# Rows padded to 128 bytes, and weights at a chosen address modulo 128, in a two-layer trunk on one core

## The chip, the core and the metric

The kernel runs on one core of one Trainium2 chip. The metric is the time of one execution on the device in microseconds (us). Three runs of the kernel before are shown; their median is compared.

## What is computed

Two layers of a decoder trunk over 256 positions of width 1024, in float32. Cut to what matters here:

```python
for l in range(2):
    h = rms_norm(x, norm_mix_pre[l])
    q, k, v, lru_x, lru_gate, glu_in, gates = split(h @ w_in[l])   # 1024 -> 11776
    y_a = dilated_attention(q, k, v) @ w_o_attn[l]     # 3 groups x 8 heads x 64
    y_b = rg_lru(lru_x, lru_gate) @ w_o_lru[l]
    y_c = conformer_conv(glu_in) @ w_o_conv[l]         # depthwise, 31 taps
    x = x + rms_norm((g0*y_a + g1*y_b + g2*y_c) @ w_out[l], norm_mix_post[l])
    u = square(relu(rms_norm(x, norm_mlp_pre[l]) @ w_mlp_up[l]))   # 1024 -> 4096
    x = x + rms_norm(u @ w_mlp_down[l], norm_mlp_post[l])
```

## The kernel before

**Products in three passes.** Each operand of a large product is split into a high part, rounded to the type fp32r (a cast on ScalarE, `act` with Copy, L392), and the remainder (a subtraction on VectorE, `tt`, L405). A product is then high x high, high x low and low x high: three matmuls, all issued at L452 in `matmuls`. Each brings its own load of the stationary operand.

**The stream of weights.** All weight matrices lie in memory as 92 chunks of 1 MiB a layer (128 partitions x 2048 float32). `weights` (L483) takes the next: a DMA on SP's queue into `raw` (two buffers), then `split` in two halves into `whi` and `wlo` (a ring of three buffers each, 8192 bytes a partition). One chunk feeds 48 matmuls of 256 columns or 24 of 512.

**Two forms of product.** In the gemm form (`ws_items`, `gemm`) the weights are the stationary operand, 128 x 128, and the activations move, 256 columns: `lx`, `glu`, `lg`, `q`, `k`, `ga`, `gb`, `gc`, `ob`, `oa`, `oc` and `up`. In the `as` form (`as_items`, `as_gemm`, `vproj`) the activations are stationary and the weights move, 512 columns: `v`, `wo`, `ua` and `dn`. For `v1` and `v2` (the dilated groups) the stationary operand takes every second element. The gates of the recurrent branch (`psr`, `psi`) are of the gemm form, but their weights are split into ordinary slots.

**Where tiles lie.** Three pools follow each other in on-chip memory: `cp` (constants and parameters), `wp` (the weight rings), `sp` (all else). A tile is placed when it is first used, at a multiple of 32 bytes. Activations lie in `hh` and `hl` (the normed input, high and low) or in the 24 slots with tag `s2` (2048 bytes each). In the program as built the first tile of `cp` is at 16512, `raw`, `whi` and `wlo` begin at 32 modulo 128, and `hh`, `hl` and all `s2` slots at 96 modulo 128; the rows of `whi`, `wlo`, `hh`, `hl` and `s2` are multiples of 128 bytes, so this holds for each buffer of a ring.

**One held chunk.** At the end of the first layer `dn61` is called with `spread`: its weights go into eight `s2` slots instead of the rings, half of its matmuls run with the first 128 positions and half later with the other 128. These matmuls have both operands in slots.

**The order of the work.** `Sched.run` simulates the engines with costs written by hand (`op(eng, cost, ...)`, costs by element counts), picks by priority, and emits all instructions in one static order per engine. `ORDER`, `CONV_AT` and `WHERE` (L38 to L44) place the chunks, the convolution's taps and the attention scores. Costs depend on a view's number of elements, not on addresses. The main matmuls follow each other in the order of the chunks; score, transpose and attention matmuls are put in between.

Of the kernel before, what the change touches and what calls it, by code (L numbers as in the profile page):

```python
# [8 lines left out]
F32R = mybir.dt.float32r  # L9
# [4 lines left out]
P = 128  # L14
# [5 lines left out]
CHUNK = 2048  # L20
# [26 lines left out]
def chunk_plan():  # L47
    q0, k0, v0, lx0, lg0, gl0, br0 = 0, 1536, 3072, 4608, 5632, 6656, 8704
    plan = []

    def ws(name, mat, c0, c1=None):
        plan.append((name, "ws", mat, (c0, c0 + P if c1 is None else c1)))

    for n in ORDER:
        kind, a = n[:2], n[2:]
        if n[0] == "v":
            for kb in range(2):
                plan.append((f"{n}{kb}", "as", "w_in", (kb, v0 + int(n[1]) * 512)))
        elif n[0] in "qk":
            plan.append((n, "rope", "w_in", (q0 if n[0] == "q" else k0) + int(n[1]) * 512 + int(n[2]) * 256))  # L60
        elif kind == "gl":
            ws(n, "w_in", gl0 + int(n[3]) * P, gl0 + D + int(n[3]) * P)
        elif kind == "oa":
            plan.append((n, "oa", "w_o_attn", int(a) * 512))
        elif kind != "lw":
            mat, c0 = {"lx": ("w_in", lx0), "lg": ("w_in", lg0), "ga": ("w_in", br0), "gb": ("w_in", br0 + D),
                       "gc": ("w_in", br0 + 2 * D), "ob": ("w_o_lru", 0), "oc": ("w_o_conv", 0)}[kind]
            ws(n, mat, c0 + int(a) * 256)
    for c in range(2):
        for kb in range(2):  # L70
            plan.append((f"wo{c}{kb}", "as", "w_out", (kb, c * 512)))
    for kb in range(9):
        if kb == 0:
            plan += [(f"ua{k}", "as", "w_mlp_up", (k, 0)) for k in range(2)]
        elif kb < 8:
            ws(f"up{2 * kb}", "w_mlp_up", (2 * kb) * 256)
            ws(f"up{2 * kb + 1}", "w_mlp_up", (2 * kb + 1) * 256)
        if kb > 0:
            for c in range(2):
                plan.append((f"dn{kb - 1}{c}", "as", "w_mlp_down", (kb - 1, c * 512)))  # L80
    return plan
# [11 lines left out]
NHI = 3  # L93
# [7 lines left out]
DMA_RATE = 0.36  # L101
MARGIN = 15000
DMA_ISSUE, DMA_START, DMA_DONE = {"SP": 600, "POOL": 1040, "ACT": 600}, 500, 900
RINGS = ("mm", "tp", "sc", "raw", "whi", "wlo", "upad", "xp", "sm", "pT")


class Buf:
    def __init__(self, sch, pool, shape, dt, tag, name):
        self.sch, self.pool, self.shape, self.dt, self.tag, self.name = sch, pool, shape, dt, tag, name
        self.t = None  # L110
        self.log = []
        self.left = 0
        self.held = False
        self.uses = []

    def __getitem__(self, idx):
        if not isinstance(idx, tuple):
            idx = (idx,)
        reg, n = [], 1
        for i, d in enumerate(self.shape):  # L120
            e = idx[i] if i < len(idx) else slice(None)
            if isinstance(e, int):
                reg.append((e, e + 1))
            else:
                r = range(*e.indices(d))
                reg.append((r[0], r[-1] + 1))
                if i:
                    n *= len(r)
        return View(self, tuple(reg), n, lambda t: t[idx])
# [3 lines left out]


class Part:
    def __init__(self, buf, off):
        self.buf, self.off = buf, off

# [12 lines left out]
class View:  # L151
# [10 lines left out]
    def ap(self):  # L162
        b = self.buf
        if b.t is None:
            b.t = b.pool.tile(list(b.shape), b.dt, tag=b.tag, name=b.name, bufs=b.sch.cap[b.tag])
        return self.fn(b.t)

    @property
    def psum(self):
        return self.buf.tag in ("mm", "tp", "sc")  # L170


class Op:
# [8 lines left out]
class Sched:  # L182
# [45 lines left out]
    def run(self):  # L228
# [4 lines left out]

        for tag in RINGS:
            ring, c = self.rings[tag], self.cap[tag]
# [117 lines left out]
def trunk_kernel(ctx: ExitStack, tc: tile.TileContext, x_d, pos_d, w_d, lruw_d, par_d, gain_d, const_d, id_d, out_d):  # L353
    nc = tc.nc
    cp = ctx.enter_context(tc.tile_pool(name="cp", bufs=1))
    wp = ctx.enter_context(tc.tile_pool(name="wp", bufs=1))
    sp = ctx.enter_context(tc.tile_pool(name="sp", bufs=1))
    pp = ctx.enter_context(tc.tile_pool(name="pp", bufs=1, space=bass.MemoryType.PSUM))
    S = Sched()
# [4 lines left out]
    def slot(name, dt=F32, shape=(P, 2, T)):  # L364
        return S.buf(sp, shape, dt, "s2", name, NSLOT)
# [41 lines left out]
    def stt(out, a, s, b, op0, op1):  # L407
        return S.op("DVE", 1.042 * out.n + 68 + 61 * aps(s),
                    lambda: nc.vector.scalar_tensor_tensor(out=out.ap(), in0=a.ap(), scalar=val(s), in1=b.ap(),  # L409
                                                           op0=op0, op1=op1), [a, b] + views(s), [out])  # L410
# [13 lines left out]
    def dma(eng, out, in_, nbytes):  # L424
        def fn():
            o = out.ap() if isinstance(out, View) else out
            i = in_.ap() if isinstance(in_, View) else in_
            eng.dma_start(out=o, in_=i)

        e = {id(nc.gpsimd): "POOL", id(nc.scalar): "ACT"}.get(id(eng), "SP")  # L430
        o = S.op(e, DMA_ISSUE[e], fn, views(in_), views(out))
        o.dma = nbytes / DMA_RATE / 1e3
        return o
# [40 lines left out]
    def split(hi, lo, src, scale=None):  # L474
        if scale is None:
            return act(hi, src, AF.Copy), tt(lo, src, hi.f32(), OP.subtract)
        return (act(hi, src, AF.Copy, scale=scale),
                stt(lo, src, scale, hi.f32(), OP.mult, OP.subtract))

    CIDX = {p[0]: n for n, p in enumerate(chunk_plan())}  # L480
    used = [0, 0]

    def weights(l, name, spread=False):  # L483
        c = CIDX[name]
        assert c == used[l], (name, c, used[l])
        used[l] += 1
        nm = f"{name}_{l}"
        raw = S.buf(wp, (P, CHUNK), F32, "raw", f"raw_{nm}", NRAW)
        if l or c:
            o = dma(nc.sync, raw.all(), w_d[l * NCH + c], CHUNK * P * 4)  # L490
            if l == 0 and c in late:
                S.follow(o, late[c])
        else:
            for s in range(2):
                o = dma(nc.sync, raw[:, s * HALF:(s + 1) * HALF], w_d[0][:, s * HALF:(s + 1) * HALF], HALF * P * 4)
                if ORDER[0][0] == "v":
                    S.follow(o, x1_load)
        if spread:
            hs, ls = [], []
            for q in range(4):  # L500
                hs.append(slot(f"whi_{nm}{q}", F32R, (P, 512)))
                ls.append(slot(f"wlo_{nm}{q}", F32R, (P, 512)))
                for o in split(hs[q].all(), ls[q].all(), raw[:, q * 512:(q + 1) * 512]):
                    o.prep = True
            return [(Quarters(hs[2 * s:2 * s + 2]), Quarters(ls[2 * s:2 * s + 2])) for s in range(2)]
        hi = S.buf(wp, (P, CHUNK), F32R, "whi", f"whi_{nm}", NHI)
        lo = S.buf(wp, (P, CHUNK), F32R, "wlo", f"wlo_{nm}", NHI)
        n = HALF if l == 0 and c < 2 else PREP
        for b in range(0, CHUNK, n):
            for o in split(hi[:, b:b + n], lo[:, b:b + n], raw[:, b:b + n]):  # L510
                o.prep = True
        return [(Part(hi, s * HALF), Part(lo, s * HALF)) for s in range(2)]
# [196 lines left out]
    for l in range(L):  # L709
# [49 lines left out]
        def glu(i):  # L759
            w = weights(l, f"glu{i}")  # L760
            ps = mm_ps(f"glu{i}_{l}")
            gemm(f"glu{i}", w, ps, hr)
            if i % 2 == 0:
                upad[i // 2] = S.buf(sp, (P, 2, 288), F32, "upad", f"upad{i}_{l}", 4)
                memset(upad[i // 2][:, :, 0:30], 0.0)
            u2 = upad[i // 2]
            th = slot(f"gth{i}_{l}", shape=(P, T))
            act(th.all(), ps[:, 1, :], AF.Tanh, scale=0.5)
            stt(u2[:, i % 2, 30:30 + T], th.all(), 1.0, ps[:, 0, :], OP.add, OP.mult)
            if i % 2 == 1:  # L770
                conv_pair(i // 2)
# [25 lines left out]
        def lg(j):  # L797
            w = weights(l, f"lg{j}")
            ps = mm_ps(f"lg{j}_{l}")
            gemm(f"lg{j}", w, ps, hr)  # L800
            q = slot(f"gq{j}_{l}")
            act(q.all(), ps.all(), AF.Square, scale=0.044715 ** 0.5)
            stt(q.all(), q.all(), 1.0, ps.all(), OP.add, OP.mult)
            act(q.all(), q.all(), AF.Tanh, scale=0.7978845608028654)
            g = slot(f"gel{j}_{l}")
            stt(g.all(), q.all(), 1.0, ps.all(), OP.add, OP.mult)
            gel[j] = g
# [319 lines left out]
        for t in range(2):  # L1127
            nm = f"pm{l}{t}"
# [79 lines left out]
        for t in range(2):  # L1208
            nm = f"pd{l}{t}"
# [100 lines left out]
```

## Time and profile before

| | |
|---|---|
| runs shown | 1140.57, 1144.45, 1145.39 us; median 1144.45 us |
| profiled execution | span 1141.4 us from the first to the last instruction; of its own time the page gives the span alone, 3.05 us under the median |
| TensorE, matmuls | 1118.9 us busy (98%), 8258 |
| VectorE | 904.4 us (79%), 1374 instructions |
| ScalarE | 720.9 us (63%), 1173 |
| DMA | 209.76 MB, mean 184 GB/s |

Matmuls overlap one another in the records, since each is drawn with its way through the array: a matmul of 256 columns is shown with some 280 ns while the next one starts after less than 120. So the distance between starts tells the pace, and the busy time does not.

### The profile page before, as it was taken

The numbers are of one execution on the slowest core, as the hardware profiler recorded it, in microseconds if no ns is written. First come the engines' busy times: TensorE is split into PE (matmuls) and PEld (weight loads), VectorE is DVE, ScalarE is ACT, GpSimd is POOL, SyncE is SP. The second block draws the span as 40 slices with busy tenths as digits, with TensorE's granted clock in tenths as the row PEclk, the third lists the DMA queues.
The fourth block names the chain that finished last, engine by engine and source line by source line (L and its number), as shares of the span: only waits on it lengthen the run. The fifth ranks groups of instructions, "written<-read, shape, count | busy, mean of one in ns | idle before, by whom it ended". The sixth has DMA issues, their size and how long they took to land.

```text
span 1141.4 us, 20586 instructions
## 1 busy us (share of the span) xinstructions
PE 1118.9 (98%) x8258; PEld 1038.8 (91%) x8258; DVE 904.4 (79%) x1374; ACT 720.9 (63%) x1173; POOL 76.3 (7%) x168
## 2 busy tenths in 40 slices
PE   7999999999999999999999999999999999999995
PEld 6999999999999899989889999999998988889984
DVE  6999999999869865555579999999995888555552
ACT  5779938687765464444468896569776646444441
POOL 1000022111000010000010000221200001000000
PEclk9999999999999999999999999999999999999998
DMA  8654376554345565554455443755624365545541
GB/s 291 237 203 149 146 244 208 185 180 146 129 180 190 186 220 185 184 185 185 184 200 207 168 184 128 252 201 194 214 90 174 136 240 185 187 183 188 193 173 37
DMA packets 37649, 209.76 MB, mean 184 GB/s; under 512 B 6449, under 2 KB 9777, under 8 KB 14130
## 3 DMA queue, kind: packets, MB, share of 16 engines
q1 hardware_dynamic: 32976, 200.05, 49.0%
q0 software_dynamic: 4576, 8.40, 2.2%
q8 instruction: 65, 1.06, 0.4%
q14 instruction: 30, 0.25, 0.1%
q10 hardware_dynamic: 2, 0.00, 0.0%
HBM read 201.08 MB, written 1.05 MB: 177 GB/s over the span
## 4 chain that ended last, share of the span: by engine, by line
PE 83%; DVE 8%; DMA 4%; ACT 3%; issue 1%; SPq 1%; POOL 0%; DVEq 0%; POOLq 0%; ACTq 0%
PE dn L452 16%; PE up L452 14%; PE glu L452 8%; PE v L452 6%; PE gc L452 4%; PE ga L452 4%; PE oc L452 4%; PE lx L452 4%; PE wo L452 4%; PE lg L452 4%; PE k L452 3%; PE oa L452 2%; PE ua L452 2%; PE ob L452 2%; PE pv L452 1%; PE tp L459 1%
## 5 line engine op out<-in xcount | busy, mean ns | idle before, releaser
L405 DVE TENSOR_TENSOR wlo_dn<-raw_dn,whi_dn 128x1024 fp32r<-128x1024 f32 (+1 forms) x66 | 75.8, 1189 | 70.2 <-ACT whi_dn L392 70.2
L392 ACT CAST whi_dn<-raw_dn 128x1024 fp32r<-128x1024 f32 (+1 forms) x66 | 64.4, 1022 | 77.2 <-PE dn L452 45.1
L409 DVE SCALAR_TENSOR_TENSOR c<-upad,parh,c 128x256 f32<-128x256 f32 x256 | 110.3, 477 | 0.1
L452 PE MATMUL up<-hh_mlp,whi_up 128*128 128x256 f32 x448 | 107.7, 280 | 0.0
L452 PE MATMUL up<-hl_mlp,whi_up 128*128 128x256 f32 x448 | 107.6, 279 | 0.0
L452 PE MATMUL dn<-whi_dn,uh 128*128 128x512 f32 x256 | 101.0, 395 | 0.0
L452 PE MATMUL dn<-wlo_dn,uh 128*128 128x512 f32 x256 | 100.8, 394 | 0.0
L405 DVE TENSOR_TENSOR wlo_up<-raw_up,whi_up 128x1024 fp32r<-128x1024 f32 x56 | 66.4, 1221 | 41.6 <-ACT whi_up L392 41.6
L399 ACT ACTIVATE cpd<-upad,parh 128x256 f32<-128x256 f32 x224 | 94.5, 500 | 3.3 <-DVE c L405 3.3
L452 PEld LDWEIGHTS up<-hh_mlp,whi_up 128*128 128x128 f32 x448 | 84.1, 188 | 0.7
L452 PEld LDWEIGHTS up<-hl_mlp,whi_up 128*128 128x128 f32 x448 | 84.0, 188 | 0.6
L392 ACT CAST whi_up<-raw_up 128x1024 fp32r<-128x1024 f32 x56 | 56.2, 1049 | 39.0 <-PE dn L452 21.0
L452 PE MATMUL dn<-whi_dn,ul 128*128 128x512 f32 x256 | 71.6, 394 | 0.0
L405 DVE TENSOR_TENSOR cpd<-cpd 128x1024 f32<-128x1024 f32 (+2 forms) x84 | 63.3, 773 | 0.9 <-ACT cpd L399 0.9
L452 PE MATMUL glu<-hl_mix,whi_glu 128*128 128x256 f32 x256 | 61.7, 279 | 0.0
L452 PE MATMUL glu<-hh_mix,whi_glu 128*128 128x256 f32 x256 | 61.7, 279 | 0.0
L452 PE MATMUL up<-hh_mlp,wlo_up 128*128 128x256 f32 x448 | 61.6, 279 | 0.0
L452 PEld LDWEIGHTS dn<-whi_dn,ul 128*128 128x128 f32 x256 | 47.9, 187 | 11.8
L452 PEld LDWEIGHTS dn<-whi_dn,uh 128*128 128x128 f32 x256 | 47.9, 187 | 11.1
L452 PEld LDWEIGHTS dn<-wlo_dn,uh 128*128 128x128 f32 x256 | 47.9, 187 | 11.0
L452 PEld LDWEIGHTS up<-hh_mlp,wlo_up 128*128 128x128 f32 x448 | 56.5, 188 | 0.0
L452 PEld LDWEIGHTS glu<-hh_mix,whi_glu 128*128 128x128 f32 x256 | 48.0, 188 | 0.0
(306 smaller groups left out, 3399.4 us busy)
## 6 DMA issues: line engine op xcount, KB each, us to landing
raw_dn<-w_in_stream SPq DMA_DIRECT2D x32, 1024.0 KB, 4.8
raw_up<-w_in_stream SPq DMA_DIRECT2D x28, 1024.0 KB, 4.8
raw_glu<-w_in_stream SPq DMA_DIRECT2D x16, 1024.0 KB, 4.8
raw_q<-w_in_stream SPq DMA_DIRECT2D x12, 1024.0 KB, 4.9
raw_k<-w_in_stream SPq DMA_DIRECT2D x12, 1024.0 KB, 4.8
raw_v<-w_in_stream SPq DMA_DIRECT2D x11, 1024.0 KB, 4.8
raw_lx<-w_in_stream SPq DMA_DIRECT2D x8, 1024.0 KB, 4.8
raw_lg<-w_in_stream SPq DMA_DIRECT2D x8, 1024.0 KB, 4.8
```

The lines of the kernel that those rows point to most:

```text
L392: nc.scalar.copy(out.ap(), in_.ap())
L399: nc.scalar.activation(out.ap(), in_.ap(), func, scale=val(scale), **kw)
L405: lambda: nc.vector.tensor_tensor(out=out.ap(), in0=a.ap(), in1=b.ap(), op=op), [a, b], [out])
L409: lambda: nc.vector.scalar_tensor_tensor(out=out.ap(), in0=a.ap(), scalar=val(s), in1=b.ap(), op0=op0, op1=op1), [a, b] + views(s), [out])
L452: nc.tensor.matmul(out.ap(), lhsT=lhs.ap(), rhs=rhs.ap(), start=start, stop=stop)
L459: nc.tensor.transpose(out.ap(), a.ap(), ident.all().ap())
```

## The change

Every tile outside PSUM, but for the single-element tiles with tag `st`, gets its last dimension padded until a row is a multiple of 128 bytes; where that adds elements, the kernel uses the slice without them (`home`). The `whi` and `wlo` buffers get 128 bytes more, and a chunk begins 16 elements (64 bytes) into them if it is used in the gemm form or by `v1` or `v2`, and at 0 if it is of the `as` form otherwise (`Shifted`). The held chunk keeps its slots.

```diff
+LINE = 128
+PSUM_TAGS = ("mm", "tp", "sc")
+UNPADDED = PSUM_TAGS + ("st",)
...
+    def home(self):
+
+        shape, row = list(self.shape), 4
+        for d in shape[1:-1]:
+            row *= d
+        last = shape[-1]
+        while self.tag not in UNPADDED and row * shape[-1] % LINE:
+            shape[-1] += 1
+        t = self.pool.tile(shape, self.dt, tag=self.tag, name=self.name, bufs=self.sch.cap[self.tag])
+        return t if shape[-1] == last else t[(slice(None),) * (len(shape) - 1) + (slice(0, last),)]
...
+class Shifted:
+    def __init__(self, buf, off):
+        self.buf, self.off = buf, off
+
+    def __getitem__(self, idx):
+        return self.buf[idx[0], idx[1].start + self.off:idx[1].stop + self.off]
...
-            b.t = b.pool.tile(list(b.shape), b.dt, tag=b.tag, name=b.name, bufs=b.sch.cap[b.tag])
+            b.t = b.home()
...
+    KIND = {p[0]: p[1] for p in chunk_plan()}
...
-        hi = S.buf(wp, (P, CHUNK), F32R, "whi", f"whi_{nm}", NHI)
-        lo = S.buf(wp, (P, CHUNK), F32R, "wlo", f"wlo_{nm}", NHI)
+        off = 0 if KIND[name] == "as" and name[:2] not in ("v1", "v2") else LINE // 8
+        hi = Shifted(S.buf(wp, (P, CHUNK + LINE // 4), F32R, "whi", f"whi_{nm}", NHI), off)
+        lo = Shifted(S.buf(wp, (P, CHUNK + LINE // 4), F32R, "wlo", f"wlo_{nm}", NHI), off)
```

Tiles whose rows the padding lengthens: `nhalf`, `halfpi`, `parh`, `const`, `n4sp`, `p2sp` and the other small tiles of `softplus`, `xp`, `cve` and `crt`.

## Rows read from the trace of the kernel before

**Rows 1.** The page, parts 1 and 2: busy time, tenths in 40 slices.
```profile
span 1141.4 us, 20586 instructions
PE 1118.9 (98%) x8258; PEld 1038.8 (91%) x8258; DVE 904.4 (79%) x1374; ACT 720.9 (63%) x1173; POOL 76.3 (7%) x168
PEclk9999999999999999999999999999999999999998
```

**Rows 2.** The chain that ended last: shares of the span by engine (page) and line.
```profile
PE 83%; DVE 8%; DMA 4%; ACT 3%; issue 1%; SPq 1%; POOL 0%; DVEq 0%; POOLq 0%; ACTq 0%
...
by line: PE dn L452 15.7%; PE up L452 13.8%; PE glu L452 7.9%; PE v L452 5.6%; PE gc L452 4.1%; PE ga L452 4.0%; PE oc L452 4.0%; PE lx L452 4.0%; PE wo L452 3.9%; PE lg L452 3.7%; PE k L452 2.9%; PE oa L452 2.0%; PE ua L452 2.0%; PE ob L45
```

**Rows 3.** The chain in order of time, longest pieces: start us, us, what, xcount.
```profile
30.46 28.27 PE glu L452 x240
...
367.42 21.00 PE wo L452 x90
...
459.68 11.20 PE dn L452 x48
470.88 11.30 PE up L452 x96
```

**Rows 4.** The chain in order of time, from 95 us on.
```profile
96.95 10.88 PE lg L452 x96
107.83 0.72 PE psr L452 x6
```

**Rows 5.** Timeline of PE, 561.9 to 566.3 us: start us, us, what, xcount.
```profile
562.08 0.39 PE L452 MATMUL dn<-whi_dn,uh 128*128 128x512 f32 x1
...
563.48 0.39 PE L452 MATMUL dn<-whi_dn,uh 128*128 128x512 f32 x1
...
564.86 0.39 PE L452 MATMUL dn<-whi_dn,uh 128*128 128x512 f32 x1
...
566.22 0.39 PE L452 MATMUL dn<-whi_dn,uh 128*128 128x512 f32 x1
```

**Rows 6.** The chain in order of time, 255 to 275 us.
```profile
260.70 11.04 PE v L452 x48
```

**Rows 7.** One tile's instructions, `wlo_dn` on DVE: duration in ns, min/median/max.
```profile
L405 DVE TENSOR_TENSOR wlo_dn<-raw_dn,whi_dn x66: 683/1220/1240, 405.8 to 1115.3; 128x1024 fp32r<-128x1024 f32 x62, 128x512 fp32r<-128x512 f32 x4
```

**Rows 8.** Stretches: us; PE, PEld, DVE, ACT, POOL busy (instructions); PEclk; DMA share, GB/s.
```profile
20.00:60.00 40.00, 40.00 (x322) 39.09 (x321) 36.76 (x75) 29.06 (x48) 0.10 (x1) 1.00 0.71 259
60.00:100.00 40.00, 40.00 (x343) 40.00 (x342) 38.07 (x72) 33.14 (x60) 1.43 (x5) 1.00 0.48 172
100.00:150.00 50.00, 49.93 (x440) 49.73 (x439) 49.21 (x73) 40.25 (x64) 0.00 (x0) 1.00 0.42 151
403.00:470.00 67.00, 67.00 (x435) 60.50 (x434) 39.48 (x46) 33.02 (x45) 3.68 (x4) 1.00 0.54 190
```

**Rows 9.** The chain in order of time where it leaves PE, both layers.
```profile
119.28 2.00 ACT whi_k L392 x2
...
142.53 2.35 DVE wlo_q L405 x2
...
163.53 5.69 DMA raw_q<-w_in_stream
...
196.58 6.03 DMA qk<-r1k
...
202.74 1.00 PE sc L452 x4
...
681.54 2.00 ACT whi_k L392 x2
...
767.24 0.66 PE tp L459 x4
```

**Rows 10.** Timeline of PE around the low parts of `q20`.
```profile
143.45 0.28 PE L452 MATMUL q<-hl_mix,whi_q 128*128 128x256 f32 x1
143.79 0.38 PE L452 MATMUL q<-hh_mix,wlo_q 128*128 128x256 f32 x1
```

More of the change, by code (lines that the diff above doesn't have):

```diff
@@ L169, in psum @@
     def psum(self):
-        return self.buf.tag in ("mm", "tp", "sc")
+        return self.buf.tag in PSUM_TAGS
 class Op:
```

## The prediction, made before the change was run

> **What bounds the kernel now.** I read the page's shares first [rows 1]: TensorE is busy 98% of the 1141.4 us span at a granted clock of nine tenths or more in 39 of the 40 slices (so 2.4 GHz), VectorE 79%, ScalarE 63%. Then the chain that ended last [rows 2]: 83% of it is TensorE. A busy TensorE says little about its pace, so the third view is the chain in order of time, where each piece gives microseconds and a number of matmuls; their quotient is the start-to-start distance of one.
>
> At 2.4 GHz a column takes 0.417 ns, so 256 columns could pass in 106.7 ns and 512 in 213.3. The pieces say otherwise [rows 3]: `glu` 28.27 us / 240 = 117.8 ns, `up` 11.30 / 96 = 117.7, `dn` 11.20 / 48 = 233.3, `wo` 21.00 / 90 = 233.3. Some pieces of 256 columns take less [rows 4]: `lg` 10.88 / 96 = 113.3. Nothing waits inside these pieces; every matmul pays 6.7, 11.1 or 20 ns over its columns.
>
> Now the addresses, which are facts of the program and not of the trace. Before, the `whi`/`wlo` rings begin at 32 modulo 128, the activations (`hh`, `hl` and all `s2` slots) at 96. Four arrangements can be read, S the stationary operand, M the moving one, modulo 128:
> - S 32, M 96 (gemm form): 113.3 or 117.8 ns, extra 6.7 or 11.1.
> - S 96, M 96 (`psr`, `psi`, both operands in slots): 0.72 / 6 = 120.0 [rows 4], extra 13.3.
> - S 96, M 32 (`as` form): 233.3, extra 20.0.
> - S 96, M 96 in the `as` form: the one held `dn` chunk, whose weights lie in slots. It runs right after ordinary `dn` matmuls [rows 5]: from 562.08 to 563.48 six take 1.40 us, 233.3 each; the twelve held ones take 563.48 to 566.22, 228.3 each, and the last six of these (from 564.86) 1.36 us, 226.7 each. Extra 13.3.
>
> The two equal arrangements cost the same 13.3 ns in both forms; the two at 64 apart cost 6.7 to 11.1 in one and 20 in the other. So the pair of addresses matters, and not the distance alone: exchanging the roles of 32 and 96 changed the extra. All extras but 11.1 are multiples of 6.7 ns, the time of 16 columns, which is 64 bytes of a float32 row.
>
> **What the change does, part by part.** The order of instructions, their number, shapes, DMAs and waits stay: the planner sees costs and element counts, and neither changes. The first tile of the pools lies at 16512 = 129 x 128, and all rows become multiples of 128 bytes, so all operands begin at 0 modulo 128 and the shifted weights at 64. Three edits count.
>
> 1. `as` form (`dn`, `wo`, `ua`, `v0`): S 96, M 32 becomes S 0, M 0. Nearest row: the held chunk, equal addresses, 226.7 ns. Their shares of the chain are 15.7 + 3.9 + 2.0% and a third of the 5.6% of `v` [rows 2]: 23.5% of 1141.4 = 268 us. 6.6 of 233.3 ns is 2.8%: **7.6 us**. Bounds: nothing, or the full 20 ns (8.6%, 23 us).
>
> 2. gemm form: S 32, M 96 becomes S 64, M 0, still 64 apart, but now each moving row of 1024 bytes fills whole pieces of 64 bytes where it began in the middle of one. Pieces at 117.8 are nearly all of `up` 13.8, `glu` 7.9, `gc` 4.1, `ga` 4.0, `oc` 4.0, `lx` 4.0, `oa` 2.0 [rows 2]: 39.8%, 454 us (some at 113.3 in `up` and `ga` stand against some at 117.8 in `k` and `ob` that I leave out). 117.8 is the only pace that is no multiple of 16 columns; I read it as two streams that meet out of step, and take that aligned starts leave the pace of 113.3. 4.5 of 117.8 ns is 3.8%: **17.3 us**. Bounds: full rate (9.4%, 43 us), or the 120.0 of `psr` (1.9% worse, 8.5 us).
>
> 3. `v1`, `v2`: S 96 with every second element, M 32 becomes S 0, M 64. They are at 11.04 / 48 = 230.0 ns [rows 6], two thirds of the `v` share, 42 us; between 226.7 and 233.3 that is 0.6 us either way, taken as 0.
>
> The rest goes together at nothing: padding (`xp`, `parh`, `const`, small tiles) adds no instruction, and the two small parameter tiles become strided for a few operations at the start. VectorE's splits (1220 ns each [rows 7]) and ScalarE's casts read and write at other addresses. No row shows them at two alignments; if that is worth 20 ns either way, VectorE has 27 us of 67 free in the MLP [rows 8], and only where it is full, 100 to 150 us (49.2 of 50), would some 18 splits cost or give 0.4 us.
>
> **What takes some back.** From 119.3 to 202.7 us the chain is not on TensorE [rows 9]: it goes through ScalarE's casts, VectorE (`wlo_q` at 142.5), DMAs of `raw_q` and `qk`, and returns at `sc`; layer 1 does the same from 681.5 to about 767. A quicker TensorE gives nothing there and waits longer at `q20`, whose first low part starts 0.34 us after the last high one, at 143.79, where 0.11 is the pace [rows 10]. The gain before 119 (72 us of gemms at 117.8 x 3.8% = 2.7 us) has to pass through VectorE, which was idle 3.2 + 1.9 + 0.8 us between 20 and 150 [rows 8]. Some of that idle time is waiting that TensorE causes, and shrinks with it; I charge 1 us a layer: **-2 us**. Next late after the change: VectorE's `wlo_q` in both layers.
>
> Sum against the profiled execution: 1141.4 - 7.6 - 17.3 + 2 = 1118.5. The median of the runs shown, 1144.45, is 3.0 over that span: **1121 us**.
>
> The Trainium skill speaks against this sum: "TensorE: Matmul & The Clock Gate", Part 2, says TensorE has two independent read ports, so that loading the next weights takes no bandwidth from the running matmul; and "SBUF — State Buffer", Specifications (TRN2), gives lines of 16 bytes, which addresses at 32 and 96 fill already. By these two the change would be worth nothing. The trace agrees only in part: [rows 5] show 6.6 ns between two arrangements of the same matmul.
>
> **Rivals.**
> - *Distance alone counts.* The gemms keep 64 apart and their mix of two paces; only edit 1 pays: 1144.5 - 7.6 = **1137**. For it: edit 1 is the one with a direct row. Against: the unlike extras at 64 apart.
> - *A piece less everywhere.* If starting inside a 64-byte piece costs one more piece per stream, aligned starts take 6.7 ns from each pace seen: gemms of 117.8 to 111.1 (5.7% of 454 us, 25.8), those of 113.3 to 106.7 (`lg` and `k`, 6.6%, 75 us, 4.4), `as` to 220 (5.7% of 268, 15.3): 45.5, less 3 us a layer at VectorE, whose idle time is then used up: **1105**; with full rate everywhere some 1085.
> - *Nothing.* What [rows 5] show comes from something other than the address: **1144**. The page's rule above is this case.
> - *Slower: the gemms meet head on.* Both streams begin on a boundary in the same instant, and the gemms get the 120.0 of `psr`: 8.5 on the pieces at 117.8, 4.4 on `lg` and `k`, 2 where the pieces between 119 and 203 us make TensorE late, less 7.6 of edit 1: +7.3, **1152**. It decides from a gemm pace of about 119 on. For it: `psr` shows that a pair of addresses can be worse than both paces of now. Against: it has its operands at one address, the gemms stay 64 apart.
>
> By itself, "TensorE: Matmul & The Clock Gate" of the Trainium skill, Part 1 (56 ns, not 53.3 ns), gives N / 2.4 GHz plus about 2.5 ns for back-to-back matmuls: 109.2 and 215.8, with which the second rival would give an estimated 1094. No row here reaches that.
>
> **The numbers.** Forecast 0.35, a piece less 0.20, distance alone 0.15, nothing 0.10, slower 0.20. About 0.5% (5.7 us) is what a measurement of this kernel can tell from no change: faster is below 1138.7, which takes the first two and somewhat more than half of the third, 0.65; within, 0.15; slower, 0.20. The range 1094 to 1150 takes in the forecast, the second rival without its end at full rate, distance alone and nothing, and leaves out most of the slower case. Within the faster cases alone it would be 1094 to 1138.
>
> **What would show it.** Right: `glu` and `up` pieces of the chain at 10.88 us per 96, `dn` at 10.88 per 48, no 117.8 left; instruction counts equal; the chain between 119 and 203 us unchanged. Wrong: `dn` still at 233 (edit 1), two gemm paces left (edit 2), 120 or more (the slower case), 111 or less (a piece less); a wait at `q20` longer by more than 2 us says that I priced VectorE's cover too low.

## The result, and the profile after

The changed kernel takes 1129.47 us (median of four runs, 1128.12 to 1131.45) against 1142.76 us of the kernel before (four runs, 1140.57 to 1145.39): ratio 0.9891, 95% interval 0.9868 to 0.9913. That is 13 us faster, where the prediction had 23. The profiled execution after is the run of 1128.12 us with a span of 1126.3, 15.1 us under the span before.

The page of the kernel after, parts 1 and 2 (busy time; tenths in 40 slices) and the shares of its chain by engine:

```profile
span 1126.3 us, 20586 instructions
...
PE 1101.3 (98%) x8258; PEld 1025.4 (91%) x8258; DVE 903.2 (80%) x1374; ACT 719.7 (64%) x1173; POOL 76.4 (7%) x168
...
PEclk9999999999999999999999999999999999999998
...
PE 81%; DVE 7%; DMA 4%; ACT 4%; issue 1%; SPq 1%; POOL 0%; DVEq 0%; POOLq 0%; ACTq 0%
```

Number and kind of instructions are those of [rows 1], and so are the page's slices of the clock. Of the busy times TensorE's fell by 17.6 us and no other by more than 1.2, and the chain is nearly the same mixture as in [rows 2]. So the time came from the pace of the matmuls, which the chain in order of time shows (start us, us, what, xcount; L476 is the line that was L452):

```profile
30.83 27.20 PE glu L476 x240
...
94.99 10.88 PE lg L476 x96
105.87 0.72 PE psr L476 x6
...
360.76 20.73 PE wo L476 x90
...
407.63 11.06 PE dn L476 x48
418.69 11.31 PE up L476 x96
...
441.08 10.90 PE up L476 x96
451.97 11.01 PE dn L476 x48
462.98 11.08 PE up L476 x96
...
485.12 11.31 PE up L476 x96
```

Divide as in [rows 3, 4]. `glu` went from 117.8 to 113.3 ns, `lg` stayed at 113.3, `psr` at 120.0. `dn` went from 233.3 to between 229.4 and 230.4, `wo` from 233.3 to 230.3. The odd one is `up`: 117.8, 113.5, 115.4, 117.8, and so on in threes. The operands of `up` are the same tiles in each chunk but for the buffers of `whi` and `wlo`, a ring of three. Two chunks of `up` and two of `dn` take turns, so the pair of buffers that `up` meets repeats after three pairs: something that differs **from buffer to buffer** sets the pace, and the change was not meant to make buffers differ.

It does. In the program as built the buffers of `whi` lay at 56352, 64544 and 72736, 8192 bytes apart. The 128 bytes that the change adds to each make that 8320: 57216, 65536, 73856, with `wlo` 24960 bytes behind `whi`. All are still equal modulo 128, but modulo 256 they alternate.

The part of the chain that is not on TensorE (compare [rows 9]):

```profile
140.84 2.35 DVE wlo_q L429 x2
...
194.44 5.56 DMA qk<-r1k
...
200.14 0.70 PE sc L476 x4
```

These stations are among those of [rows 9]; `sc` comes 2.6 us earlier than before.

### The profile page after: what moved, and what is told of

The parts are those of the page before. It is cut to its first block, busy times and chain, and to the rows that moved or that the text cites. A ratio compares the mean times of both kernels' runs of the same rounds, so it can differ in the third digit from the quotient of the medians.

```text
span 1126.3 us, 20586 instructions
## 1 busy us (share of the span) xinstructions
PE 1101.3 (98%) x8258; PEld 1025.4 (91%) x8258; DVE 903.2 (80%) x1374; ACT 719.7 (64%) x1173; POOL 76.4 (7%) x168
## 4 chain that ended last, share of the span: by engine, by line
PE 81%; DVE 7%; DMA 4%; ACT 4%; issue 1%; SPq 1%; POOL 0%; DVEq 0%; POOLq 0%; ACTq 0%
PE dn L476 15%; PE up L476 14%; PE glu L476 8%; PE v L476 5%; PE gc L476 4%; PE ga L476 4%; PE wo L476 4%; PE lx L476 4%; PE oc L476 4%; PE lg L476 4%; PE k L476 3%; PE ua L476 2%; PE oa L476 2%; PE ob L476 2%; PE pv L476 1%; PE tp L483 1%
## 5 line engine op out<-in xcount | busy, mean ns | idle before, releaser
L476 PE MATMUL up<-hh_mlp,whi_up 128*128 128x256 f32 x448 | 106.3, 278 | 0.0
L476 PE MATMUL up<-hl_mlp,whi_up 128*128 128x256 f32 x448 | 106.0, 278 | 0.0
L476 PE MATMUL dn<-wlo_dn,uh 128*128 128x512 f32 x256 | 100.5, 393 | 0.0
L476 PE MATMUL dn<-whi_dn,uh 128*128 128x512 f32 x256 | 100.4, 392 | 0.0
L476 PEld LDWEIGHTS up<-hl_mlp,whi_up 128*128 128x128 f32 x448 | 84.3, 188 | 0.6
L476 PEld LDWEIGHTS up<-hh_mlp,whi_up 128*128 128x128 f32 x448 | 84.2, 188 | 0.6
L476 PE MATMUL dn<-whi_dn,ul 128*128 128x512 f32 x256 | 70.8, 392 | 0.0
L476 PE MATMUL up<-hh_mlp,wlo_up 128*128 128x256 f32 x448 | 60.7, 278 | 0.0
L476 PE MATMUL glu<-hh_mix,whi_glu 128*128 128x256 f32 x256 | 59.6, 276 | 0.0
L476 PE MATMUL glu<-hl_mix,whi_glu 128*128 128x256 f32 x256 | 59.6, 276 | 0.0
L476 PEld LDWEIGHTS dn<-whi_dn,ul 128*128 128x128 f32 x256 | 48.0, 188 | 10.8
L476 PEld LDWEIGHTS dn<-wlo_dn,uh 128*128 128x128 f32 x256 | 48.0, 188 | 10.4
L476 PEld LDWEIGHTS dn<-whi_dn,uh 128*128 128x128 f32 x256 | 48.1, 188 | 10.3
L476 PEld LDWEIGHTS up<-hh_mlp,wlo_up 128*128 128x128 f32 x448 | 55.7, 188 | 0.0
L476 PEld LDWEIGHTS glu<-hh_mix,whi_glu 128*128 128x128 f32 x256 | 48.0, 188 | 0.0
```

The costliest lines, as they stand in the source:

```text
L476: nc.tensor.matmul(out.ap(), lhsT=lhs.ap(), rhs=rhs.ap(), start=start, stop=stop)
```

## The experiments

Two theories stood against each other. **Alignment**, the prediction's reading: it matters where in a 64-byte piece the operands start. **Distance and pitch**: only the difference between the two addresses matters, and the pitch, the 8320 bytes from buffer to buffer, is part of the cause. Each ratio below is to the kernel before, run on the same chip.

### Shift without a choice of form, and shift without padded rows

The first run keeps rows and shift, but shifts all chunks alike:

```diff
-        off = 0 if KIND[name] == "as" and name[:2] not in ("v1", "v2") else LINE // 8
+        off = LINE // 8
```

> Rows padded to 128 bytes as in the change, but every chunk begins 64 bytes in, so that the as form stays 64 apart from its activations. Theory 'distance' (only the distance of the two operands modulo 128 sets the paces): dn back at 233.3 ns, time within 4 us of the kernel before plus what the gemms' mix of 113.3 and 117.8 happens to be. Theory 'absolute' (where an operand begins within 128 bytes counts by itself): the gemms show the mix of the changed kernel, about three quarters at 113.3, and the time lies some 6 to 8 us below before.

Measured: 1130.05 us, ratio 0.9894 [0.9872, 0.9915], the whole gain of the change without its edit 1. `dn` is at 231 to 232 ns although stationary and moving operand are 64 apart again (modulo 128; modulo 256 the buffers now lie 64 or 192 apart).

The second run leaves rows unpadded (the two lines of padding in `home` are gone) and moves the `as` chunks instead of the others:

```diff
-        off = 0 if KIND[name] == "as" and name[:2] not in ("v1", "v2") else LINE // 8
+        off = LINE // 8 if KIND[name] == "as" and name[:2] not in ("v1", "v2") else 0
```

> No row is padded (operands at 32 and 96 modulo 128 as before); only the weights of the as form begin 64 bytes later, at the address of the activations modulo 128. Theory 'distance': dn at 230.4 as in the changed kernel, gemms' mix as in the changed kernel, time within 3 us of it (1127 to 1133). Theory 'absolute': dn quicker, but glu and up at 117.8 as before, time about 6 us below before, 1136 to 1138.

Measured: 1128.93 us, ratio 0.9878 [0.9857, 0.99], again the whole gain, with no row padded. So what both runs share is the likely cause, and they share the pitch of 8320.

### Padded rows and weights at 64, pitch 8192 as before

```diff
-        hi = Shifted(S.buf(wp, (P, CHUNK + LINE // 4), F32R, "whi", f"whi_{nm}", NHI), off)
-        lo = Shifted(S.buf(wp, (P, CHUNK + LINE // 4), F32R, "wlo", f"wlo_{nm}", NHI), off)
+        hi = S.buf(wp, (P, CHUNK), F32R, "whi", f"whi_{nm}", NHI)
+        lo = S.buf(wp, (P, CHUNK), F32R, "wlo", f"wlo_{nm}", NHI)
```

A tile of 64 bytes ahead of the `whi` ring puts all weights at 64 modulo 128, and one behind the `wlo` ring puts the activations back at 0.

> Rows padded, all weights at 64 modulo 128, activations at 0, and the ring buffers again 8192 bytes apart instead of 8320: both distances and pitch are those of before, only the absolute addresses differ. Theory 'distance': nothing differs from before, dn 233.3, glu and up 117.8, within 0.3%. Theory 'absolute': as the run with rows alone. Theory 'pitch' (the distance of the ring buffers from one another disturbs the streams): this run equals before while the run with rows alone does not.

Measured: 1143.03 us, ratio 1.0016 [1.0003, 1.0028]. Its chain has the paces of before to the hundredth of a microsecond:

```profile
30.42 28.27 PE glu L480 x240
...
411.88 11.20 PE dn L480 x48
423.08 11.30 PE up L480 x96
```

Here every gemm has S 64, M 0, the addresses that edit 2 was to gain from, and nothing is gained. **Alignment falls**, and with it the first of the prediction's readings.

### The two forms alone, at chosen addresses

> Leaves out the whole computation: it runs trains of 96 gemm matmuls (256 columns) and 48 as matmuls (512 columns) from four resident tiles, with no other engine busy, each train with the operands at chosen bytes modulo 128 (stationary at 0, 16 ... 112 against moving at 0; the old pair 32/96 and 96/32; the equal pair 96/96; low parts 128 bytes further), three times over. Theory 'distance': g_old equals g_e (64 apart, 113.3 or 117.8), g_mid equals g_a (120), m_old equals m_e (233.3), m_mid equals m_a (226.7). Theory 'absolute': g_e below g_old, m_a below m_mid. Theory 'pitch': m_far, whose low parts lie 128 bytes further, shows 230 to 231 where m_a shows 226.7; without it both are equal. If the extras come from other engines' traffic, all trains run at 106.7 and 213.3.

From the chain of that run, its first repetition (trains without a wait inside; `g_` is the gemm form, `m_` the `as` form). The stationary operand starts so many bytes past the moving one: `g_e` 64, `g_old` 32 against 96, `g_mid` 96 against 96, `g_far` 64 with the low parts 128 bytes further; `m_a` 0, `m_old` 96 against 32, `m_far` 0 with the low parts 128 further:

```profile
66.96 11.32 PE g_e L71 x96
...
117.43 11.32 PE g_old L71 x96
129.98 11.53 PE g_mid L71 x96
...
142.75 10.91 PE g_far L71 x96
...
154.89 10.91 PE m_a L71 x48
...
216.77 11.21 PE m_old L71 x48
...
241.38 11.11 PE m_far L71 x48
```

These pieces hold a little of their train's start; inside, the starts are 117.8 ns apart for `g_e` and `g_old`, 120.0 for `g_mid` (both operands at 96) and for `g_a`, 113.3 for `g_far`; 226.7 for `m_a`, 233.3 for `m_old`, 231.0 for `m_far`. In this repetition equal distances give equal paces wherever the operands lie, and `g_old`, 192 apart modulo 256, has the pace of `g_e`, 64 apart. Two things are new. `m_far` says that the `as` form loses most of its gain if only the low parts lie 128 bytes further. And `g_e` was at 117.8 in the first repetition and at 113.3 in the other two, `g_far` at 113.3, 117.8 and 113.3, **with the same addresses**: a gemm train 64 apart has two paces and, inside these trains, keeps the one it has.

### The pitch alone

The kernel before with 128 bytes more in each `whi` and `wlo` buffer and nothing else (`off = 0`, rows unpadded).

> The kernel before with nothing but 128 bytes more in each whi and wlo buffer: rows unpadded, weights at 32 and activations at 96 modulo 128 as before, the buffers of a ring 8320 bytes apart where they were 8192. Theory pitch: the 128 bytes that the change adds to each buffer carry most of its gain, so this alone gives 1130 us (1127 to 1133), with three quarters of the gemm matmuls at 113.3 ns and dn at about 231. Rival, shift and rows needed together with it: no gain by itself, 1143, dn at 233.3 and most gemms at 117.8.

Measured: 1126.97 us, ratio 0.9875 [0.9857, 0.9893]. So the 128 extra bytes alone, which were only to make room for the shift, give all that the change gives. Counted from the starts in the records, 4988 of the gemms' matmuls are at 113.3 ns, against 1798 before and 4525 in the changed kernel. Its chain and, in the timeline of PE, the first third of one `up`:

```profile
421.50 10.95 PE up L474 x96
```

```profile
421.33 0.28 PE L474 MATMUL up<-hh_mlp,whi_up 128*128 128x256 f32 x1
...
423.22 1.07 PE L474 MATMUL up<-hh_mlp,wlo_up 128*128 128x256 f32 x8
...
425.94 1.07 PE L474 MATMUL up<-hh_mlp,wlo_up 128*128 128x256 f32 x8
```

The 16 matmuls with high parts, from 421.33 to 423.22, take 118.1 ns each. The next 24, 8 with low parts and 16 with high ones, take 2.72 us, 113.3 each. The train changed its pace where it changed from `whi` to `wlo`.

### Low parts brought back in step with high parts; all at distance 0; pairs of trains

`even_rings` puts 640 bytes between the two rings of the changed kernel, so that `wlo` lies 25600 bytes, a multiple of 1024, behind `whi`:

```diff
+        if self.tag == "wlo" and "ahead" not in self.sch.cap:
+            self.sch.cap["ahead"] = self.pool.tile([P, 160], F32, tag="ahead", name="ahead", bufs=1)
```

> The changed kernel with 640 bytes between the whi ring and the wlo ring, so that each low part lies a multiple of 1024 bytes behind its high part; everything else as changed, pitch 8320. Theory high-low distance: the as form lost the 226.7 ns of equal addresses because its moving operand alternates between whi and wlo at addresses that differ by 384 modulo 512; with that gone dn is at 226.7 (10.88 us per 48 against 11.05), 268 us x 1.5% = 4 us less than the change. If the gemms keep their mix, 1125; if the gemms' fast pace comes from the irregular starts of the as form before them, it goes with them, and up returns to 117.8: then 1129 to 1137. Rival, the pitch from one buffer to the next is what matters to the as form: dn stays at 230, 1129.

Measured: 1134.78 us, ratio 0.9938 [0.9924, 0.9953]. The gemms lost most of their gain, as one of the two cases in the expectation has it, but `dn` did not go to 226.7; with 230 it is where the rival puts it. Its chain:

```profile
420.48 11.30 PE up L478 x96
431.79 11.04 PE dn L478 x48
```

and the timeline of PE, first matmul of this `dn`, of its second chunk, and of the `up` behind it:

```profile
431.62 0.40 PE L478 MATMUL dn<-whi_dn,uh 128*128 128x512 f32 x1
...
437.07 0.40 PE L478 MATMUL dn<-whi_dn,uh 128*128 128x512 f32 x1
...
442.67 0.28 PE L478 MATMUL up<-hh_mlp,whi_up 128*128 128x256 f32 x1
```

The first 24 take 5.45 us, 227.1 ns each, the other 24 take 5.60, 233.3 each. The first chunk lies in the buffer at 65536, equal to the activations modulo 256; the second in one that is 128 off. So equal modulo 128 is not enough for the `as` form: it has to be **equal modulo 256**. Over all `dn` and `wo` matmuls of this kernel, the mean is 228.2 ns for 0 modulo 256 and 232.6 for 128.

`all_zero` has `off = 0` for every chunk of the changed kernel; at the pitch of 8320 the distance is then 0 or 128 modulo 256.

> The changed kernel with every chunk at 0 in its buffer: all weights and all activations at 0 modulo 128, pitch 8320. Theory distance: the gemms pay the 120.0 ns of equal addresses, as trains with nothing else running and psr showed; against before's mean of about 116.5 that is 3%, some 20 us of 680, less 4 us in the as form at 230, so 1155 to 1163; dn 230. Rival, absolute alignment or the pitch keeps the gemms at 113 to 118 whatever the distance: 1125 to 1135.

Measured: 1149.92 us, ratio 1.0078 [1.0061, 1.0095], slower, though by less than expected, since the gemms did not all go to 120.0:

```profile
31.21 28.60 PE glu L476 x240
...
427.94 11.46 PE up L476 x96
```

`glu` is at 119.2 ns and `up` at 119.4; over all gemms the mean is 119.7 at distance 0 and 118.4 at 128. So distance 0, the best of the `as` form, is the worst of the gemm form; the change is right not to treat them alike.

> Leaves out the whole computation: pairs of trains of matmuls with nothing else running, the second right behind the first. An as train at equal addresses whose low parts lie 0, 128, 256, 384, 512, 640, 768 or 1024 bytes further than the high ones, then a gemm train 64 apart with the same distance of its low parts. Theory high-low distance: as is at 226.7 ns for 0 and 1024, and slower, 230 to 232, for others, the gemm train is at 113.3 or 117.8 as it is entered: 113.3 behind the irregular trains, 117.8 behind the regular ones. Rival 1, the gemm pace is set by the distance of its own low parts: the same value in each of three repetitions for a distance. Rival 2, chance: both values turn up for one pair. The pair with the addresses of before (96 and 32) is expected at 233.3 and 117.8, and with 384 added at 231 and 113.3; a gemm train behind one at equal addresses (120.0) at 117.8.

From its chain, in the first repetition: pairs with low parts 128 and 256 bytes further (`a_f` is the `as` train, `b_f` the gemm train behind it), then the addresses of before (`old`), then those with 384 added (`oldp`):

```profile
42.44 11.10 PE a_f L73 x48
53.53 10.91 PE b_f L73 x96
66.53 10.92 PE a_f L73 x48
77.45 11.32 PE b_f L73 x96
...
212.02 11.19 PE a_old L73 x48
223.20 11.32 PE b_old L73 x96
236.62 11.15 PE a_oldp L73 x48
247.77 10.98 PE b_oldp L73 x96
```

In this repetition the `as` train is at 226.7 for multiples of 256 and at 231.0 for odd multiples of 128, and the gemm train is at 117.8 behind the first and at 113.3 behind the second. In the other two repetitions some trains hold stretches at 1.2 GHz, and there three pairs with odd multiples had the gemm train at 117.8 in one or both; both values turn up for one pair, as rival 2 (chance) has it. What holds in all repetitions: no multiple of 256 was followed by 113.3, and the addresses of before never were. Rival 1 is out, since one distance gave both paces.

It is less chance than it looks, for at odd multiples of 128 the `as` train has two paces as well. The pair with 384 in the third repetition, at the full clock:

```profile
725.41 11.01 PE a_f L73 x48
736.42 11.32 PE b_f L73 x96
```

Its `as` train is at 229.1 ns. In all nine pairs with odd multiples the gemm train was at 113.3 behind an `as` train at 231.0 (four pairs) and at 117.8 behind one at 229.1 (five). What chooses between 231.0 and 229.1 was not shown.

### What makes a train change its pace

Each matmul's addresses are known from the program, its start from the trace. I took the unbroken trains of gemms (12 or more matmuls, no two starts more than 124 ns apart) of seven kernels, and the distance, stationary minus moving, modulo 256. Before, it is 192 everywhere. With pitch 8320 it is 192 in some buffers and 64 in others, so a train crosses from 192 to 64 at some steps from `whi` to `wlo`, or to the next buffer.

```
                  trains without a crossing      trains with one
                  all 113  all 118  changed      all 113  all 118  118 to 113
before               22       50       0            -        -        -
rows_pitch           11       60       0            -        -        -
even_rings           14       36       0            4        9        8
the change           15       13       0           14       12       17
rows_only            15       13       0           13        8       22
as_shift_only        18       15       0           12        3       23
pitch_only           19       14       0           11        3       24
```

All 94 changes go from 117.8 to 113.3, each within four matmuls behind a crossing; none goes back, and none of the 315 trains without a crossing changed. A crossing does not always work. The first four starts of a train are not counted: 38 of the 172 trains without a crossing in the last five rows begin with up to four slower starts, 115 to 123 ns, and then stand at 113.3, and all 38 begin at distance 64, none at 192.

The run with pairs of trains has the same change with nothing else running. In `b_oldp` the distance goes from 192 to 64 at each step from high to low parts; in two of three repetitions it began at 117.8 and changed behind the first such step:

```profile
247.61 0.28 PE L73 MATMUL b_oldp<-ah,wh 128*128 128x256 f32 x1
...
249.49 1.09 PE L73 MATMUL b_oldp<-ah,wl 128*128 128x256 f32 x8
250.41 0.28 PE L73 MATMUL b_oldp<-ah,wh 128*128 128x256 f32 x1
...
252.00 0.28 PE L73 MATMUL b_oldp<-ah,wh 128*128 128x256 f32 x1
```

The first 16 take 1.88 us, 117.5 ns each, and the 14 from 250.41 on 1.59 us, 113.6. Nine trains of that run that began at 117.8 have the step from 192 to 64 from low to high parts instead, and none of them changed. All this was counted after the fact, so it was put to a test.

### The test: as form at 0 modulo 256, with and without a crossing

Both kernels have unpadded rows and buffers 8448 bytes apart, a multiple of 256. They differ in the low parts of the gemm weights alone (`low` is the offset in `wlo`):

```diff
-        off, low = (LINE // 8, LINE // 8) if KIND[name] == "as" and name[:2] not in ("v1", "v2") else (0, 0)
+        off, low = (LINE // 8, LINE // 8) if KIND[name] == "as" and name[:2] not in ("v1", "v2") else (0, 0 if KIND[name] == "as" else LINE // 4)
```

> The kernel before, rows unpadded, with buffers 8448 bytes apart (a multiple of 256), weights of the as form moved by 64 bytes: all of its operands at equal addresses modulo 256, in all buffers and for high and low parts alike; the gemms stay at 192 modulo 256 (stationary minus moving) as before. Theory modulo 256: this is edit 1 of the prediction without the shift from buffer to buffer: dn is at 226.7 ns throughout (10.88 us per 48, 21.76 per 96), and no gemm leaves the pace at which its train starts, so most of them are at 117.8, up all of it: 1141 - 7.6 = 1134 (1132 to 1138). Rival, the as form stays irregular for another reason: dn 229 to 231, 1137 to 1139 with gemms at 117.8, or 1127 if they fall to 113.3 behind it.

> As the kernel labelled meant, and in the gemm form the low parts of the weights start 128 bytes further into their buffers, so that the distance goes from 192 to 64 modulo 256 at each step from the high parts to the low parts, three times in a train of 72 and twice in 48. Theory crossing: a gemm train leaves 117.8 for 113.3 only where the distance goes from 192 to 64, and never goes back unbroken; so up starts at 117.8 behind the regular dn and is at 113.3 from the first or second step to the low parts on (10.9 to 11.1 us per 96), while dn stays at 226.7: 1134 less 15 for the gemms, 1120 (1117 to 1124), below both kernels. Rival, the gemms got 113.3 because the as form before them ended out of step: with a regular dn they stay at 117.8 and this is at 1134 as well. Rival, the crossing costs something by itself: 1127 or more.

> The changed kernel once more, beside the kernel labelled steered on the same chip: both theories expect 1129 (1128 to 1132), a ratio of 0.989 to before.

Measured: without a crossing (`meant`) 1135.77 us, ratio 0.9944 [0.993, 0.9958]; with it (`steered`) **1123.53**, ratio 0.9848 [0.9826, 0.987]; the change again 1131.13, 0.9903 [0.9885, 0.9922]. The chain of the first:

```profile
412.43 10.89 PE dn L474 x48
423.32 11.30 PE up L474 x96
```

and of the second:

```profile
410.44 10.90 PE dn L474 x48
421.34 11.08 PE up L474 x96
```

`dn` is at 226.9 and 227.1 ns. `up` is at 117.7 in all chunks without a crossing, and at 115.4 with it: with the first 44 of a train at 117.8 and the other 52 at 113.3 it comes to 11.08 us. Of 71 trains without a crossing none changed its pace; with one, 23 of 36 changed, 22 of them four matmuls behind a step from high to low parts, and 11 were at 113.3 from the start. `steered` beats both kernels: its interval ends below that of the change on the same chip, and no row of it is padded. Its profiled execution is the longest of the five, 1130.04 us; TensorE's granted clock in it was 1.2 GHz from 178.1 to 185.0 us, beginning in a wait of 3.1 us at `sc`. The paces above are read outside that stretch.

## Why the prediction was right in direction and wrong in size

**Reading of the bound: right.** TensorE's pace was the place where the time was; no count of instructions changed, and the stations of the chain that are shown stayed [rows 1, 9]. Of what was to show the forecast wrong, "two gemm paces left" came.

**Edit 1, 7.6 us: the term was mis-sized at 3.3.** The row it came from, the held chunk at 226.7 ns [rows 5], is confirmed by `meant`: all of `dn` at 226.9, and 1135.77 against 1141.83 is 6.1 us, which is edit 1 less the loss of 268 gemms at 113.3 (1.2 us). The step that failed is "the held chunk has equal addresses, so equal addresses modulo 128 give 226.7". The held chunk lies in slots 2048 bytes apart and was equal modulo 256 too; the rings at a pitch of 8320 are not. The changed kernel got 230.4 in the mean: (233.3 - 230.4) / 233.3 x 268 us = 3.3.

**Edit 2, 17.3 us: the cause was wrong, and the term came to 12.1.** "Aligned starts leave the pace of 113.3" fell with the run that had the aligned starts and the old pitch (1143.03). What came instead came by the pitch: 4525 - 1798 = 2727 more matmuls at 113.3, 4.45 ns each, 12.1 us. That the gemms gained at all was luck: the same aligned addresses at the old pitch gave nothing, and the pitch changed only because the shift needed room. I noticed that the gemms have two paces at one pair of addresses [rows 3, 4], and took the slower one for a meeting of two streams out of step. That was near; but the pair of paces in [rows 4, 3] said that the addresses alone don't decide, and I priced it as if they did. I also read the change's 128 more bytes as room for the shift and followed only addresses modulo 128, where the ring's pitch cancels.

**"The pair of addresses matters, and not the distance alone": wrong.** In the runs of both forms alone, equal distances gave the same paces wherever the operands lay; what I took for a matter of the pair was that the two forms answer to a distance in opposite ways: 0 is the best of one and the worst of the other.

**VectorE's take-back, 2 us: 1.5 of it showed, all in layer 1.** Layer 0 gave nothing back: `sc` came 2.6 us earlier than before while `lg` had come 2.0 earlier [rows 4, 9], and the wait at `q20` is 0.34 us as in [rows 10]. In layer 1 the kernel before goes on to its first `sc` without a wait, and the changed one waits 1.53 us there; before, then after:

```profile
741.46 1.18 PE L452 MATMUL sc<-qk 64*128 64x256 f32 x12
```

```profile
730.42 0.83 PE L476 MATMUL sc<-qk 64*128 64x256 f32 x6 [1.53 <-DVE mx L964]
```

The other six kernels that beat the one before have this wait too, 0.8 to 2.4 us, and `rows_pitch` and `all_zero` do not. Between 20 and 100 us VectorE was idle for 3.24 + 1.93 us before [rows 8] and is idle for 2.17 + 0.80.

The terms give 3.3 + 12.1 = 15.4 us against 15.1 between the spans, though 1.5 was lost to the wait at `sc`, because the profiled execution before lost about as much to the clock, which the digits of [rows 1] hide. Behind the wait at `sc` of 202.74 its granted clock was 1.2 GHz for a stretch (columns as in [rows 8]; the 0.51 is the mean of this window), with matmuls 213 ns apart:

```profile
203.00:206.40 3.40, 3.40 (x17) 3.17 (x17) 3.34 (x7) 1.76 (x2) 0.00 (x0) 0.51 0.50 205
```

Up to the fifth matmul of `ob` these instructions took 3.63 us, and 2.16 after the change, where the clock stayed up: some 1.5 us that the change did not earn. Of the forecast's miss, 1126.3 - 1118.5 = 7.8 us, edit 1 makes 4.3 and edit 2 5.2; a take-back 0.5 us smaller than charged and the 1.5 us of clock stand against it.

**v1, v2 at nothing: right.** They were at 230.0 [rows 6] and are at 230 to 232.

**Rivals.** *Distance alone* came nearest to the rule, though the distance counts modulo 256 and not 128, and by it 1137; `meant`, which is that case, took 1135.77. *Nothing* is what aligned rows are worth (1143.03). There the row agrees with "SBUF — State Buffer" of the Trainium skill, Specifications (TRN2), whose 16-byte lines were filled before. *A piece less* has no trace: no pace under 113.3 or 226.7 was seen. *Slower* has its mechanism in `all_zero`, 119.2 to 119.4 ns and 1149.92, at equal addresses modulo 128 and not at 64 apart.

The same matmuls at 226.7 and 233.3, or 117.8 and 120.0, by the distance between stationary and moving operand speak against the second rule that I had weighed, "TensorE: Matmul & The Clock Gate" of the Trainium skill, Part 2, by which loading weights takes nothing from the running matmul. No run here has matmuls without a load of their own, so what the load itself costs was not separated.

**What stays open.** Why 256 bytes, why a gemm train has two paces, and why a crossing works only in one direction and not always, was not shown. That the pace of an `as` train sets the pace at which the gemms behind it start is suggested by the nine pairs of trains, 231.0 with 113.3 and 229.1 with 117.8, and not settled.

## What to carry to other kernels

When a change touches where tiles lie, follow every address that it moves, the pitch of each ring too, and at more than one modulus: here the padding that made room for a shift did more than the shift. Where one instruction shows two paces at the same addresses, find what selects the pace before you price it. Test the parts of a layout change one at a time, since each costs only a line.

## What the runs showed of the hardware that was not expected

- The pace of matmuls with a weight load each depends on the distance, stationary minus moving. 512 columns: 226.9 ns at 0 modulo 256 (`meant`), 232.6 at 128 (`even_rings`), 233.3 at 64 (before); 230.4 where high and low parts alternate between 0 and 128 (the change). By themselves, such trains ran at 231.0 or at 229.1 at the same addresses.
- 256 columns: 120 ns at distance 0, 118.4 at 128 (`all_zero`), and 117.8 or 113.3 at 64 or 192. From its fifth start on a train keeps its pace; it went from 117.8 to 113.3 only behind a step from 192 to 64, in 117 of 117 changes over the kernels of the table and `steered`, and never back.
- Operands at 64 and 0 modulo 128 with padded rows, in place of 32 and 96, gained nothing at equal distances and pitch (`rows_pitch`, ratio 1.0016 [1.0003, 1.0028]).
